# Raising the scheduling priority of turned-operand splits and of softmax normalising in a two-layer encoder trunk

## The chip, the cores and the metric

The kernel runs on one core of one Trainium2 chip. A core has five engines with a queue each: PE (TensorE, matmuls and transposes; PEld is its weight load), DVE (VectorE), ACT (ScalarE), POOL (GpSimd) and SP (SyncE, which issues transfers here). The metric is the device time of one execution in microseconds (us); lower is better. The time before is the median of three runs, 1124.85 us (1124.82 to 1125.47).

## What is computed

Two layers of a bidirectional encoder in float32, for 512 tokens of width 1024 and a memory of 256 rows. Each layer adds a normalised mixer and a normalised SwiGLU feed-forward network to x. The mixer has 12 token heads (3 key/value heads, 4 query heads on each) and 4 heads that attend to the memory. Layer 0 is banded attention within 128 tokens with a sink logit per head; layer 1 is full attention with normalised queries and keys and a rotary by row and column.

```
def reference(x, mem, ...):
    mem_n = rms_norm(mem, mem_norm_g)
    for i in range(DEPTH):                       # DEPTH = 2
        h = rms_norm(x, g_mix_pre[i])
        proj = h @ w_in[i]                       # q (768), k (192), v (192), qm (256)
        ...
        tok = mixer_a(q, k, v, sink, ...) if kind == 0 else mixer_b(q, k, v, qk_g, ...)
        mo = memory_attention(qm, km, vm)        # softmax(qm km^T / 8) vm over 256 rows
        o = jnp.concatenate([tok, mo], axis=-1) @ w_o[i]
        x = x + rms_norm(o, g_mix_post[i])
        h = rms_norm(x, g_ffn_pre[i])
        gu = h @ w_gate_up[i]
        f = (jax.nn.silu(gu[..., :D_FF]) * gu[..., D_FF:]) @ w_down[i]   # D_FF = 2816
        x = x + rms_norm(f, g_ffn_post[i])
    return x
```

## The kernel before

**Products.** Tokens are cut into four tiles of 128. Every float32 product is made of three products of a rounded form: `mm3` (L267) adds high by high, high by low and low by high. So each operand exists as a pair hi, lo. `split` (L274) makes it: ACT copies the source into hi with rounding (L280), then DVE subtracts hi from the source to give lo (L284). For some weights a flag sends hi (L278) or lo (L282) to POOL. In the profile all these splits have the lines 278 to 284, and the tile names tell them apart: whi and wlo are weights, th and tl turned probabilities or the split token output, q the split queries, a the turned rows of the feed-forward network.

**Turned operands.** A matmul contracts over partitions, so rows must be transposed first. PE transposes 128x128 blocks into a PSUM tile `tp` (tag "t", two buffers), and a split reads them out. There are three such places: `turned` (L330 and on, transposes L337) for the rows of a mixer's input, `Forms.turn` (transposes L149) for the feed-forward network, whose first products are made from sums of blocks (`Forms` keeps a1, a21, a22 and the sums S1 to S4), and `turn` (transposes L609) for a head's probabilities, which gives th and tl.

**A head.** Heads are counted through both layers here: 0 to 15 in layer 0, 16 to 31 in layer 1, the last four of each being memory heads. `score` computes the scores of one token tile (L548, L549), a row extreme nm (DVE, L554 in layer 0, L559 in layer 1), and exponentials with their sum den (ACT, L560). `score_mem` does the same for the memory heads, for two tiles at once (L578 to L580, exponentials L583). After the last tile `normalise` adds the sink term (es, L594), takes the reciprocal rd (L596) and multiplies the four tiles' probabilities p by it on POOL (L599). Then `turn` j transposes the block of keys j from all tiles that see these keys: in layer 0, j = 0 needs tiles 0 and 1 only; in layer 1 every turn needs all four. `value` multiplies th and tl by the values into one PSUM bank o (tag "pv", one buffer; L623, L624). After the last j, ACT copies half of o to tmp (L631), DVE adds the other half into tok (L632), and only then may the next head write o. The queries of the next group of four heads are projected meanwhile: the copy out of PSUM is qx (ACT, L512), a rotary follows on DVE (L423 to L444), a split gives q, its transposes are L524 and their copy qT is L525. tok is split into th (L280, L284) for the output projection.

**What sets the order.** PE's order is written by hand: in `mixer`, `put(x, f)` files each piece of work under a due time worked out from the table PACE, and the pieces are emitted in that order. On ACT, DVE, POOL and SP the build's scheduler arranges the instructions, from their priorities (by default the order of emission) and from when it takes their inputs to be there; each engine then runs its own list in order. `tc.high_priority(n)` moves the instructions emitted inside it forward by n in the scheduler's priorities.

Of the kernel before, what the change touches and what calls it, by code (L numbers as in the profile page):

```python
# [12 lines left out]
AF = mybir.ActivationFunctionType  # L13
OP = mybir.AluOpType
# [17 lines left out]
WPART = 2  # L32
BIG = 1e37
NFILL = 3
LOTS = ((0, 8), (8, 14), (14, 22))

PACE = [{'lag': 1.692, 'vlag': 0.479, 'jstep': 0.213, 'kstep': 0.375, 'klag': 0.742, 'qoff': [0.212, 0.126, 0.099], 'qlag': 1.02, 'late': 0.6, 'moff': -0.235, 'mdur': 0.562, 'mlag': 0.697, 'kw': [0, 0, 2, 0], 'mw': [2, 1, 1, 0], 'qw': [1, 0, 0, 1, 3, 3, 3, 3], 'hoff': 0, 'ow': [10.3, 10.8, 12.2, 13.2], 'ox': 11.4, 'od': 0.3, 'hstep': 0.872, 'hlag': 1.742, 'hjstep': 0.135, 'hvlag': 0.751, 'owm': [0, 0, 0, 0, 0, 0, 0, 0], 'q0step': 0.27, 'q0off': -0.032, 'q0lag': 0.919, 'm0off': -0.078, 'm0dur': 0.002, 'm0lead': 1.887, 'mlead': 1.201, 'qlead': 0.921, 'q0lead': 1.555, 'qstep': 1.002, 'tw': [0, 0, 0, 0, 0, 0, 0, 0], 'h2off': 0}, {'lag': 1.824, 'vlag': 0.535, 'jstep': 0.218, 'kstep': 0.777, 'klag': 1.715, 'qoff': [-0.027, -0.162, -0.027], 'qlag': 1.189, 'late': 2.15, 'moff': -0.088, 'mdur': 0.384, 'mlag': 1.205, 'kw': [0, 0, 0, 0], 'mw': [0, 0, 0, 0], 'qw': [0, 0, 0, 0, 0, 3, 1, 1], 'hoff': 0, 'ow': [10.2, 10.7, 12.2, 13.2], 'ox': 11.3, 'od': 0.3, 'hstep': 0.946, 'hlag': 1.847, 'hjstep': 0.295, 'hvlag': 0.568, 'owm': [0, 0, 0, 0, 0, 0, 0, 0], 'q0step': 0.718, 'q0off': -0.018, 'q0lag': 1.136, 'm0off': -1.059, 'm0dur': 0.171, 'm0lead': 2.465, 'mlead': 3.162, 'qlead': 1.895, 'q0lead': 1.42, 'qstep': 0.998, 'tw': [0, 0, 0, 0, 0, 0, 0, 0], 'h2off': 0.016}]
# [79 lines left out]
class Forms:  # L117
# [23 lines left out]
    def turn(self, t, h):  # L141
        tr, nc = self.tr, self.nc
        q, c = t // 2, slice(t % 2 * P, t % 2 * P + P)
        if q and self.s is None:
            self.new_s()
        for b in range(2):
            tp = tr.ps.tile([P, 4, P], F32, tag="t", name="tp", bufs=2)
            for k in range(4):
                nc.tensor.transpose(tp[:, k], h[:, (4 * b + k) * P:(4 * b + k + 1) * P], tr.ident)  # L149
            if q == 0:  # L150
                ks = slice(4 * b, 4 * b + 4)
                tr.split(self.a1[0][:, ks, c], self.a1[1][:, ks, c], tp)
                nc.scalar.activation(self.as1[:, ks, c], tp, AF.Copy)
                continue
            dst = (self.a21, self.a22)[b]
            tr.split(dst[0][:, :, c], dst[1][:, :, c], tp)
            if b == 0:
                a21 = self.temp("a21", 2)
                nc.scalar.activation(a21, tp, AF.Copy)
            else:  # L160
                s1 = self.temp("s1", 2)
                nc.vector.tensor_sub(s1, tp, a21)
                self.left.append((c, a21, s1))

    def finish(self):

# [13 lines left out]
class Trunk:  # L180
# [93 lines left out]
    def split(self, hi, lo, src, pool=0):  # L274
# [8 lines left out]
        else:  # L283
            nc.vector.tensor_sub(lo, src, hi.bitcast(F32))  # L284

    def split_scaled(self, hi, lo, src, r, pool=0):

        nc = self.nc
        if pool & 2:
            nc.gpsimd.tensor_scalar(hi, src, r, 1.0, op0=OP.mult, op1=OP.mult)  # L290
        else:
            nc.scalar.activation(hi, src, AF.Copy, scale=r)  # L292
        nc.vector.scalar_tensor_tensor(lo, src, r, hi.bitcast(F32), op0=OP.mult, op1=OP.subtract)
# [38 lines left out]
    def turned(self, h, his, los, t, nq=4):  # L332

        for b in range(2):
            tp = self.ps.tile([P, 4, P], F32, tag="t", name="tp", bufs=2)
            for k in range(4):
                self.nc.tensor.transpose(tp[:, k], h[:, (4 * b + k) * P:(4 * b + k + 1) * P], self.ident)  # L337
            k0 = 4 * b
            sl = (slice(None), slice(k0 % nq, k0 % nq + 4), slice(t * P, (t + 1) * P))
            self.split(his[k0 // nq][sl], los[k0 // nq][sl], tp)  # L340

    def scale_rows(self, rs, by_row=False):

# [245 lines left out]
    def normalise(self, hd):  # L589
        nc, sink, nm, den = self.nc, hd["sink"], hd["nm"], hd["den"]  # L590
        rd = self.small.tile([P, 4], F32, tag="rd", name="rd", bufs=4)
        if sink is not None:
            es = self.small.tile([P, 4], F32, tag="es", name="es", bufs=3)
            nc.scalar.activation(es, nm, AF.Exp, bias=self.sink[:, sink:sink + 1], scale=1.0)  # L594
            nc.vector.tensor_add(den, den, es)
        nc.vector.reciprocal(rd, den)  # L596
        for z, (k0, k1) in enumerate(hd["rng"]):
            n = (k1 - k0) * P
            self.pooled = nc.gpsimd.tensor_scalar(hd["p"][z][:, :n], hd["p"][z][:, :n], rd[:, z:z + 1], 1.0,  # L599
                                                  op0=OP.mult, op1=OP.mult)  # L600

    def turn(self, hd, j):
        nc = self.nc
        qs = [i for i in range(NT) if hd["rng"][i][0] <= j < hd["rng"][i][1]]
        m = len(qs)
        tp = self.ps.tile([P, 4, P], F32, tag="t", name="tp", bufs=2)
        for z, i in enumerate(qs):
            jj = j - hd["rng"][i][0]
            nc.tensor.transpose(tp[:, z], hd["p"][i][:, jj * P:(jj + 1) * P], self.ident)  # L609
        th = self.core.tile([P, 4, P], F32R, tag="th", name="th", bufs=4)  # L610
        tl = self.core.tile([P, 4, P], F32R, tag="tl", name="tl", bufs=4)
        self.split(th[:, :m], tl[:, :m], tp[:, :m])
        hd[j] = (qs[0] * P, (qs[-1] + 1) * P, th[:, :m].rearrange("p a b -> p (a b)"),
                 tl[:, :m].rearrange("p a b -> p (a b)"))

# [149 lines left out]
    def heads_out(self, l, put, xw, xs, x0, dx):  # L765
# [7 lines left out]
        def part(k):  # L773
            if k % 4 == 0:
                self.th[k // 4] = [self.hp.tile([P, 4, S], F32R, tag=f"h{k // 4}{z}", name="th", bufs=1)
                                   for z in range(2)]
            self.split(self.th[k // 4][0][:, k % 4], self.th[k // 4][1][:, k % 4], self.tok[:, k],
                       self.side(l, "tw", k))

        def prod(k, t):  # L780
            if t == len(self.po):
                self.po.append(self.bank())
                if t == 2:
                    self.held = self.turns.pop()
            self.prod(self.po[t], self.heads, KD, k, t, self.wo[k // 2])

        for k in range(KD):
            put(max(xs[k], x0 + (NFILL * k - 1.5) * dx) if k < NH // 2 else xs[k], lambda k=k: part(k))
        for k in range(NH // 2):
            for t in range(NFILL):  # L790
                put(max(x0 + (NFILL * k + t) * dx, xs[k] + 0.001 * (t + 1)), lambda k=k, t=t: prod(k, t))

# [3 lines left out]
    def mix_out(self, l, forms, resid, dst):  # L796
# [3 lines left out]
        g, gn = self.gain(a["g_mix_post"][l], "gpost"), self.gain(a["g_ffn_pre"][l], "gpre")  # L800
        po = self.po + [self.bank() for _ in range(NT - NFILL)]
        self.turns.insert(1, self.held)
        w1 = []
        for u in range(4):
            for k in (2 * u, 2 * u + 1):
                for t in range(0 if k >= NH // 2 else NFILL, NT):
                    self.prod(po[t], self.heads, KD, k, t, self.wo[u])
# [97 lines left out]
    def ffn(self, l, pools, forms, late, done):  # L905
# [92 lines left out]
        def body(f, pos, nxt, nxt2, fill):  # L998
            d = st[f]
            x = d["x"]  # L1000
            seven(f, x, "c", 1, "S2", False)
            copy(f, "u2", x)
            y = self.tagged("t")[:, :256]
            seven(f, y, "c", 0, "nS1", True)
            copy(f, "p5", y)
            if nxt is not None:
                load_b(nxt)
                prep_c(nxt)
                p1(nxt)
            else:  # L1010
                fill[0]()
            seven(f, x, "b", 1 - 1, "S3", False)
            c = d["cc"] = temp("c")
            nc.vector.tensor_add(c[:, 256:], x, d["p5"])
            if nxt is not None:
                p2(nxt)
            else:
                fill[1]()
            if nxt2 is not None:
                prep_a(nxt2)  # L1020
            seven(f, y, "b", 1, "S4", False)
            nc.vector.tensor_add(c[:, :256], y, d["u2"])
            if nxt is not None:
                prep_b(nxt)
            seven(f, x, "d", 0, "A22", False)
            s = d["s"]
            nc.scalar.activation(s[:, 256:], x, AF.Silu)
            nc.vector.tensor_mul(s, s, c)
            F[f] = hidden(pos)
            nc.scalar.activation(F[f][0], s, AF.Copy, scale=-1.0)  # L1030
            nc.vector.scalar_tensor_tensor(F[f][1], s, -1.0, F[f][0].bitcast(F32), op0=OP.mult, op1=OP.subtract)
            if nxt is not None:
                prep_d(nxt)
            st.pop(f)
# [24 lines left out]

        for c, (f0, f1) in enumerate(LOTS):  # L1060
            fs = list(range(f0, f1))
# [21 lines left out]
            for i, f in enumerate(gs):  # L1083
                more = gs[i + 1:] + [None, None]
                body(f, f - f0, more[0], more[1], [first, second])
            if c < len(LOTS) - 1:
                self.down(get, self.a["wd"][l], fs, c, o, head)
# [158 lines left out]
```

## Time and profile before

| | |
|---|---|
| Median of the runs | 1124.85 us |
| The profiled execution, its own time | 1125.38 us |
| its span in the trace | 1123.6 us |
| PE busy | 98% |
| DVE, ACT, POOL busy | 75%, 59%, 18% |
| granted PE clock, mean | 0.998 |
| PE idle in the two mixers (20 to 200 us, 565 to 745 us) | 5.7 and 6.1 us |
| PE idle in the two feed-forward networks (225 to 545, 800 to 1124 us) | 0.0 and 8.2 us, the latter nearly all at the end of the program |

PE is the engine that sets the time. The other engines matter where PE waits for them. The list of waits gives, for each pair of a PE line and the line that released it, the idle time in all, how often, and the longest. In the timeline each row has the start, the duration, the engine and line, the operation, output and inputs, and in brackets the idle time of the engine ahead of it.

### The profile page before, as it was taken

What the parts mean: (1) busy time and instruction counts of PE and PEld (TensorE: products, weight loads), DVE (VectorE), ACT (ScalarE), POOL (GpSimd) and SP (SyncE); (2) the same over time, 40 slices, a digit from 0 to 9 for tenths busy, and PEclk for the clock granted to TensorE, in tenths of its full rate; (3) what the DMA queues carried; (4) which work ended last, traced back from release to release, by engine and by line L of the source; (5) the groups of instructions that cost most, each with busy time, mean ns of one, the idle gap of its engine ahead of it and who ended that gap; (6) DMA issues with size and microseconds to landing.
All of it is one profiled execution on the core that took longest, in us unless ns stands there. A gap on an engine that the chain in (4) does not pass through costs nothing.

```text
span 1123.6 us, 19533 instructions
## 1 busy us (share of the span) xinstructions
PE 1096.6 (98%) x7463; PEld 1003.6 (89%) x7463; DVE 844.3 (75%) x1431; ACT 660.8 (59%) x1343; POOL 203.8 (18%) x348
## 2 busy tenths in 40 slices
PE   8999999999999999999999999999999999999997
PEld 7889988899889989998898888878999899899985
DVE  5688885899557867885788998758996478669854
ACT  6678984666445634663467878756665255345631
POOL 5693331102000000000343543312000000000001
PEclk9999999999999999999999999999999999999999
DMA  6521015443753382325543221145136223423243
GB/s 237 194 81 47 20 57 206 169 132 114 243 180 112 112 283 76 112 79 195 179 150 113 76 76 39 38 150 188 39 113 217 65 76 114 149 62 103 85 166 112
DMA packets 38685, 139.29 MB, mean 124 GB/s; under 512 B 4416, under 2 KB 4800, under 8 KB 38464
## 3 DMA queue, kind: packets, MB, share of 16 engines
q1 hardware_dynamic: 38448, 137.91, 36.4%
q8 instruction: 58, 0.95, 0.3%
q14 instruction: 35, 0.29, 0.1%
q10 hardware_dynamic: 144, 0.14, 0.0%
HBM read 119.16 MB, written 18.87 MB: 123 GB/s over the span
## 4 chain that ended last, share of the span: by engine, by line
PE 68%; DVE 6%; ACT 3%; POOL 2%; issue 2%; DVEq 0%; POOLq 0%; ACTq 0%
PE ps L978 12%; PE ps L979 12%; PE ps L980 12%; PE ps L271 9%; PE ps L270 9%; PE ps L272 9%; PE tp L609 1%; PE o L624 1%; PE o L623 1%; PE s L548 1%; DVE nm L559 1%; PE s L549 1%; DVE wlo L284 1%; POOL r L299 1%; ACT whi L280 1%
## 5 line engine op out<-in xcount | busy, mean ns | idle before, releaser
L280 ACT ACTIVATE whi<-raw 128x1024 fp32r<-128x1024 f32 (+2 forms) x186 | 157.9, 863 | 185.2 <-PE ps L980 81.8
L284 DVE TENSOR_TENSOR wlo<-raw,whi 128x1024 fp32r<-128x1024 f32 (+2 forms) x178 | 175.9, 998 | 74.8 <-ACT whi L280 71.7
L978 PE MATMUL ps<-sf,whi 128*128 128x256 f32 x640 | 179.9, 281 | 0.2
L979 PE MATMUL ps<-sf,wlo 128*128 128x256 f32 x640 | 179.7, 281 | 0.0
L980 PE MATMUL ps<-sf,whi 128*128 128x256 f32 x640 | 179.7, 281 | 0.0
L270 PE MATMUL ps<-whi,f 128*128 128x512 f32 x352 | 137.2, 390 | 0.0
L271 PE MATMUL ps<-wlo,f 128*128 128x512 f32 x352 | 137.1, 390 | 0.0
L272 PE MATMUL ps<-whi,f 128*128 128x512 f32 x352 | 137.0, 389 | 0.0
L980 PE MATMUL ps<-a,whi 128*128 128x256 f32 x480 | 134.4, 280 | 0.0
L978 PE MATMUL ps<-a,whi 128*128 128x256 f32 x480 | 134.3, 280 | 0.0
L979 PE MATMUL ps<-a,wlo 128*128 128x256 f32 x480 | 133.8, 279 | 0.0
L978 PEld LDWEIGHTS ps<-sf,whi 128*128 128x128 f32 x640 | 121.1, 189 | 1.1 <-ACT p L984 0.6
L979 PEld LDWEIGHTS ps<-sf,wlo 128*128 128x128 f32 x640 | 121.4, 190 | 0.5
L980 PEld LDWEIGHTS ps<-sf,whi 128*128 128x128 f32 x640 | 121.4, 190 | 0.0
L308 POOL TENSOR_SCALAR e<-sso 128x1 f32<-128x1 f32 x8 | 3.4, 424 | 566.1 <-ACT junk L303 565.9
L270 PE MATMUL ps<-whi,hT 128*128 128x256 f32 (+1 forms) x320 | 98.8, 309 | 0.9 <-ACT whi L292 0.9
L271 PE MATMUL ps<-wlo,hT 128*128 128x256 f32 (+1 forms) x320 | 93.9, 294 | 2.6 <-DVE wlo L284 1.9
L599 POOL TENSOR_SCALAR p<-p,rd 128x256 f32<-128x256 f32 (+2 forms) x128 | 78.2, 630 | 99.8 <-DVE rd L596 50.3
L272 PE MATMUL ps<-whi,hT 128*128 128x256 f32 (+1 forms) x320 | 93.7, 293 | 0.0
L979 PEld LDWEIGHTS ps<-a,wlo 128*128 128x128 f32 x480 | 90.5, 188 | 0.2
L978 PEld LDWEIGHTS ps<-a,whi 128*128 128x128 f32 x480 | 90.4, 188 | 0.2
L980 PEld LDWEIGHTS ps<-a,whi 128*128 128x128 f32 x480 | 90.1, 188 | 0.0
(201 smaller groups left out, 2735.0 us busy)
## 6 DMA issues: line engine op xcount, KB each, us to landing
raw<-in_wgu_dram SPq DMA_DIRECT2D x48, 512.0 KB, 4.4
raw<-in_wd_dram SPq DMA_DIRECT2D x44, 512.0 KB, 4.4
rb<-in_wgu_dram SPq DMA_DIRECT2D x40, 512.0 KB, 3.6
raw<-in_wo_dram SPq DMA_DIRECT2D x17, 512.0 KB, 3.6
raw<-in_wq_dram SPq DMA_DIRECT2D x16, 512.0 KB, 5.0
xt<-x SPq DMA_DIRECT2D x12, 512.0 KB, 4.5
raw<-in_wm_dram SPq DMA_DIRECT2D x8, 512.0 KB, 4.3
x<-y SPq DMA_DIRECT2D x8, 512.0 KB, 3.0
```

The costliest lines, as they stand in the source:

```text
L270: mm(out, lh, rh, start=first, stop=False)
L271: mm(out, lh, rl, start=False, stop=False)
L272: mm(out, ll, rh, start=False, stop=last)
L280: nc.scalar.activation(hi, src, AF.Copy)
L284: nc.vector.tensor_sub(lo, src, hi.bitcast(F32))
L299: g.tensor_tensor(r, r, self.mhalf[:, :r.shape[1]], op=OP.pow)
L548: nc.tensor.matmul(s[:, :n], qi, hd["ka"]()[:, k0 * P:k1 * P], start=True, stop=False)
L549: nc.tensor.matmul(s[:, :n], qi, hd["kb"]()[:, k0 * P:k1 * P], start=False, stop=True)
L599: self.pooled = nc.gpsimd.tensor_scalar(hd["p"][z][:, :n], hd["p"][z][:, :n], rd[:, z:z + 1], 1.0, op0=OP.mult, op1=OP.mult)
L978: mm(out, wh[:, s], rh, start=start and k == 0, stop=False, skip_group_check=True)
L979: mm(out, wl[:, s], rh, start=False, stop=False, skip_group_check=True)
L980: mm(out, wh[:, s], rl, start=False, stop=k == 3, skip_group_check=True)
```

## The change

The splits that read out transposes (in `Forms.turn`, `turned` and `turn`) and POOL's multiplies in `normalise` are put under `urgent()`, that is, under a scheduling priority raised by 400. Nothing is added to the program or taken from it. An attribute that nothing uses (`self.pooled`) goes.

```diff
+URGENT = 400
...
@@ Forms.turn
+            with tr.urgent():
+                if q == 0:
+                    ks = slice(4 * b, 4 * b + 4)
+                    tr.split(self.a1[0][:, ks, c], self.a1[1][:, ks, c], tp)
+                    nc.scalar.activation(self.as1[:, ks, c], tp, AF.Copy)
+                    continue
+                dst = (self.a21, self.a22)[b]
+                tr.split(dst[0][:, :, c], dst[1][:, :, c], tp)
...
+    def urgent(self):
+
+        return self.tc.high_priority(URGENT)
...
@@ turned
-            self.split(his[k0 // nq][sl], los[k0 // nq][sl], tp)
+            with self.urgent():
+                self.split(his[k0 // nq][sl], los[k0 // nq][sl], tp)
...
@@ normalise
-            self.pooled = nc.gpsimd.tensor_scalar(hd["p"][z][:, :n], hd["p"][z][:, :n], rd[:, z:z + 1], 1.0,
-                                                  op0=OP.mult, op1=OP.mult)
+            with self.urgent():
+                nc.gpsimd.tensor_scalar(hd["p"][z][:, :n], hd["p"][z][:, :n], rd[:, z:z + 1], 1.0, op0=OP.mult,
+                                        op1=OP.mult)
...
@@ turn
-        self.split(th[:, :m], tl[:, :m], tp[:, :m])
+        with self.urgent():
+            self.split(th[:, :m], tl[:, :m], tp[:, :m])
```

PE's list of instructions is the same before and after, row for row. In the changed kernel lines have moved on by 2 to 9: L280 is L282, L282 is L284, L284 is L286, L525 is L532, L559 is L566, L560 is L567, L583 is L590, L594 is L601, L599 is L607, L631 is L640, L632 is L641.

**POOL, heads 2 and 3 of layer 0.** rd_1168 belongs to head 2, whose p of the token tiles 0 to 3 are p_1073, p_1111, p_1136 and p_1165; wlo is the low part of a weight. Before:

```order
L282 TENSOR_TENSOR wlo_1632<-raw_1630,whi_1631 128x512
L599 TENSOR_SCALAR p_1073<-p_1073,rd_1168 128x256
L599 TENSOR_SCALAR p_1111<-p_1111,rd_1168 128x384
L599 TENSOR_SCALAR p_1136<-p_1136,rd_1168 128x384
L599 TENSOR_SCALAR p_1165<-p_1165,rd_1168 128x256
L282 TENSOR_TENSOR wlo_1632<-raw_1630,whi_1631 128x512
L599 TENSOR_SCALAR p_1215<-p_1215,rd_1291 128x256
```

With the change:

```order
L284 TENSOR_TENSOR wlo_1632<-raw_1630,whi_1631 128x512 x2
L607 TENSOR_SCALAR p_1073<-p_1073,rd_1168 128x256
L607 TENSOR_SCALAR p_1136<-p_1136,rd_1168 128x384
L607 TENSOR_SCALAR p_1111<-p_1111,rd_1168 128x384
L607 TENSOR_SCALAR p_1165<-p_1165,rd_1168 128x256
L607 TENSOR_SCALAR p_1215<-p_1215,rd_1291 128x256
```

Tiles 1 and 2 have changed places, as they have in each of the 32 heads, and the second half of the weight's split now stands ahead of head 2's multiplies.

**ACT, the end of layer 0's token heads and the first memory head.** den_2175 is the last token head, den_2274 the first memory head; raw_2395 is a weight. Before:

```order
L594 ACTIVATE es_2250<-nm_2174,sink_88 128x4
L280 ACTIVATE th_2269<-tp_2265 128x384
L280 ACTIVATE whi_2396<-raw_2395 128x512
L280 ACTIVATE th_2293<-tp_2289 128x384
L583 ACTIVATE p_2281,den_2274<-s_2275,nm_2273 128x256
L583 ACTIVATE p_2283,den_2274<-s_2275,nm_2273 128x256
L525 ACTIVATE qT_1715<-tp_2297 128x4x128
L280 ACTIVATE th_2318<-tp_2315 128x256
L280 ACTIVATE whi_2396<-raw_2395 128x512
```

With the change:

```order
L282 ACTIVATE th_2269<-tp_2265 128x384
L282 ACTIVATE whi_2396<-raw_2395 128x512
L567 ACTIVATE p_2246,den_2175<-p_2246,nm_2174 128x256
L282 ACTIVATE th_2293<-tp_2289 128x384
L601 ACTIVATE es_2250<-nm_2174,sink_88 128x4
L532 ACTIVATE qT_1715<-tp_2297 128x4x128
L590 ACTIVATE p_2281,den_2274<-s_2275,nm_2273 128x256
L282 ACTIVATE th_2318<-tp_2315 128x256
L590 ACTIVATE p_2283,den_2274<-s_2275,nm_2273 128x256
```

th_2269, th_2293 and th_2318 have moved forward, both parts of whi_2396 as well, and qT_1715 and th_2318 now stand ahead of the second exponential of the memory head.

**DVE, head 19 in layer 1.** tl_8011 belongs to this head's second turn, q2_7959 is the split of the next queries, tok_7503<-o_7918 is the end of the head before. Before:

```order
L444 TENSOR_TENSOR qx_7944<-qx_7944,r4_7950 128x256
L559 TENSOR_REDUCE nm_7992<-s_7994 128x1
L632 TENSOR_TENSOR tok_7503<-o_7918,tmp_8002 64x512
L284 TENSOR_TENSOR q2_7959<-qx_7944,q2_7959 128x4x64
L284 TENSOR_TENSOR tl_8011<-tp_8005,th_8010 128x512
L559 TENSOR_REDUCE nm_7992<-s_8026 128x1
```

With the change:

```order
L451 TENSOR_TENSOR qx_7944<-qx_7944,r4_7950 128x256
L566 TENSOR_REDUCE nm_7992<-s_7994 128x1
L286 TENSOR_TENSOR tl_8011<-tp_8005,th_8010 128x512
L286 TENSOR_TENSOR q2_7959<-qx_7944,q2_7959 128x4x64
L641 TENSOR_TENSOR tok_7503<-o_7918,tmp_8002 64x512
L566 TENSOR_REDUCE nm_7992<-s_8026 128x1
```

tl has moved from behind tok and q to the front, and tok stands behind both.

More of the change, by code (lines that the diff above doesn't have):

```diff
@@ L149, in turn @@
                 nc.tensor.transpose(tp[:, k], h[:, (4 * b + k) * P:(4 * b + k + 1) * P], tr.ident)
[L150 to L163, printed above, removed]
+            with tr.urgent():
[6 more added lines that the diff above has]
+                tr.split(dst[0][:, :, c], dst[1][:, :, c], tp)
+                if b == 0:
+                    a21 = self.temp("a21", 2)
+                    nc.scalar.activation(a21, tp, AF.Copy)
+                else:
+                    s1 = self.temp("s1", 2)
+                    nc.vector.tensor_sub(s1, tp, a21)
+                    self.left.append((c, a21, s1))
     def finish(self):
```

## The prediction

> **What bounds the kernel now.** I read the page first: how busy each engine is, then the list of what TensorE (PE) waits for, then the timeline at the places that the new order touches.
>
> ```profile
> span 1123.6 us, 19533 instructions
> PE 1096.6 (98%) x7463; PEld 1003.6 (89%) x7463; DVE 844.3 (75%) x1431; ACT 660.8 (59%) x1343; POOL 203.8 (18%) x348
> ```
>
> PE is busy for 1096.6 of 1123.6 us and its order is written by hand: nothing can be won except the 27 us in which it stands still. So the question for every moved instruction is whether PE waits for it, and what now comes later instead. The list of PE's waits names the lines (engine, line, releaser: total, times, longest):
>
> ```profile
> PE tp L609 <- DVE tl L284: 2.7, 6, 0.7
> PE o L623 <- DVE tok L632: 2.3, 5, 0.7
> PE tp L609 <- POOL p L599: 1.8, 3, 0.9
> ...
> PE o L624 <- DVE tl L284: 0.3, 2, 0.2
> ...
> PE tp L609 <- DVE qx L424: 0.2, 1, 0.2
> PE tp L524 <- ACT qx L512: 0.2, 1, 0.2
> ```
>
> The splits that the change brings forward (th on ACT, tl on DVE) are what PE waits for in the first and the fourth row: 2.7 + 0.3 us. The two qx waits (0.2 + 0.2) lie on the same queues and may move with them. That gives a **ceiling for the gain of 3.4 us**, 0.3% of the time. The second and third rows are work that the change can only delay: tok isn't raised, and the POOL multiplies are reordered.
>
> **The change part by part.** No instruction is added or removed, so each term is a change of a start time. The sum is made against the profiled execution's own 1125.38 us (span 1123.6 and 1.8 around it), which is 0.53 above the median 1124.85.
>
> *Normalising (POOL).* In each head the multiplies now run for token tiles 0, 2, 1, 3 instead of 0, 1, 2, 3. A layer 0 turn for keys j = 0 transposes tiles 0 and 1 only, so it now waits for the third multiply. Head 0 is a place where PE stands for exactly that:
>
> ```profile
> 71.08 2.23 POOL L599 TENSOR_SCALAR p<-p,rd 128x256 f32<-128x256 f32 x4
> 72.33 0.33 PE L609 MATMUL tp<-cst,p 128*128 128x128 f32 x1 [0.40 <-POOL p L599]
> ```
>
> Four multiplies take 2.23, one about 0.56: **+0.57**. In layer 1 a turn reads all four tiles, so there the swap costs nothing. Head 2 of layer 0 gets a second penalty: a POOL weight split (L282) that followed its four multiplies now stands ahead of them.
>
> ```profile
> 84.91 1.60 POOL L599 TENSOR_SCALAR p<-p,rd 128x384 f32<-128x384 f32 x3
> 86.48 1.48 POOL L282 TENSOR_TENSOR wlo<-raw,whi 128x512 fp32r<-128x512 f32 x1
> 86.51 0.38 PE L609 MATMUL tp<-cst,p 128*128 128x128 f32 x2
> 88.95 0.30 PE L609 MATMUL tp<-cst,p 128*128 128x128 f32 x1 [0.29 <-DVE tl L284]
> ```
>
> The last of these multiplies ended at 86.5 and the third at about 86.0. With 1.48 ahead, tile 1, now third, ends at about 87.5; PE asks for it at 86.62 (the second of the two at 86.51), moved to about 87.0 by the terms before it: **+0.4** (bounds 0 and 0.9). The other 29 heads have their multiplies ready early, since only three waits of PE on them are listed; cost nothing, cover gone only if rd comes over 1 us later.
>
> *Turned probabilities, gain.* The waits on tl and qx vanish at best: **−3.4**, all of it taken. The row at 88.95 above is one of them; the largest I can point at with nothing behind it is this one:
>
> ```profile
> 658.93 0.66 PE L609 MATMUL tp<-cst,p 128*128 128x128 f32 x4 [0.63 <-DVE tl L284]
> ```
>
> *Turned probabilities, what comes later.* ACT and DVE run one instruction after the other, so a th or tl that goes ahead pushes back everything that it passes. Five places in layer 0 put th ahead of the copy of q out of PSUM (L512), which frees the bank that the next q transposes (L524) write:
>
> ```profile
> 130.62 0.45 ACT L512 ACTIVATE qx<-ps,rq 128x256 f32<-128x256 f32 x1
> 130.97 0.48 ACT L280 ACTIVATE th<-tp 128x384 fp32r<-128x384 f32 x1
> 131.32 0.54 PE L524 MATMUL tp<-identr,q 128*128 128x128 f32 x4
> ```
>
> L512 ends at 131.07 with 0.25 to spare. Starts of neighbours on ACT are closer than their durations (0.35 from 130.62 to 130.97, for a 0.45), so a th of 0.48 costs some 0.37 of pace, and 0.12 to 0.2 is lost; five places with similar room, **+0.65** (bounds 0 and 1.8, five full th). Next, the end of layer 0's token heads, and the memory heads behind it:
>
> ```profile
> 137.85 0.68 DVE L632 TENSOR_TENSOR tok<-o,tmp 64x512 f32<-64x512 f32 x1
> 138.73 0.56 DVE L284 TENSOR_TENSOR tl<-tp,th 128x384 fp32r<-128x384 f32 x1 [0.20 <-ACT th L280]
> ...
> 138.59 0.39 PE L623 MATMUL o<-th,vs 128*128 128x256 f32 x1 [0.36 <-DVE tok L632]
> ...
> 146.24 0.47 ACT L583 ACTIVATE p<-s,nm 128x256 f32<-128x256 f32 x1
> ...
> 146.69 0.60 ACT L525 ACTIVATE qT<-tp 128x512 fp32r<-128x512 f32 x1
> 147.17 0.40 ACT L280 ACTIVATE th<-tp 128x256 fp32r<-128x256 f32 x1
> 147.43 0.65 ACT L280 ACTIVATE whi<-raw 128x512 fp32r<-128x512 f32 x1
> ...
> 146.87 0.37 PE L578 MATMUL s<-kma,qT 128*128 128x256 f32 x1
> ```
>
> PE already waits for tok at 138.59; with that tl ahead of it tok comes its 0.56 later, **+0.56**. At 146 the exponentials of the first memory head (L583), the second of which ends at 146.71, 0.16 ahead of the scores that need its bank, now stand behind qT, th and whi: 0.48 + 0.26 of pace from the rows and some 0.5 of the whi's 0.65, less 0.16, is 1.1. Part of it is hidden where PE is late already: **+0.7** (bounds 0.55 and 1.1). The same queue in layer 1 puts qT, a th and the split of tok ahead of the second L583:
>
> ```profile
> 709.28 0.48 ACT L583 ACTIVATE p<-s,nm 128x256 f32<-128x256 f32 x1
> ...
> 709.73 0.61 ACT L525 ACTIVATE qT<-tp 128x512 fp32r<-128x512 f32 x1
> 710.20 0.62 ACT L280 ACTIVATE th<-tp 128x512 fp32r<-128x512 f32 x1
> 710.68 0.66 ACT L280 ACTIVATE th<-tok 128x512 fp32r<-128x512 f32 x1
> ...
> 710.45 0.36 PE L578 MATMUL s<-kma,qT 128*128 128x256 f32 x1
> ```
>
> It ended at 709.76, 0.69 ahead of PE; 0.47 + 0.48 of pace and some 0.5 of the 0.66 go ahead: 1.5 less 0.69 is **+0.8**. At the first output of a memory head, tmp (L631) and tok now follow a th and a tl:
>
> ```profile
> 723.72 0.60 ACT L280 ACTIVATE th<-tp 128x512 fp32r<-128x512 f32 x1
> ...
> 723.73 0.69 DVE L632 TENSOR_TENSOR tok<-o,tmp 64x512 f32<-64x512 f32 x1 [1.17 <-ACT tmp L631]
> 724.45 0.69 DVE L284 TENSOR_TENSOR tl<-tp,th 128x512 fp32r<-128x512 f32 x1
> ...
> 724.48 0.50 PE L623 MATMUL o<-th,vm 128*128 128x512 f32 x1 [0.48 <-DVE tok L632]
> ```
>
> PE waits for tok here, and a 0.60 th or a 0.69 tl comes in front; DVE's idle 1.17 takes up a little: **+0.5**, and the same **+0.5** in layer 0, which has the same order. The last place is head 19 in layer 1, where tok moves behind tl and the split of q:
>
> ```profile
> 638.24 0.69 DVE L632 TENSOR_TENSOR tok<-o,tmp 64x512 f32<-64x512 f32 x1
> 638.97 0.82 DVE L284 TENSOR_TENSOR q<-qx,q 128x256 fp32r<-128x256 f32 x1
> 639.82 0.69 DVE L284 TENSOR_TENSOR tl<-tp,th 128x512 fp32r<-128x512 f32 x1
> ...
> 639.36 0.40 PE L623 MATMUL o<-th,vs 128*128 128x512 f32 x1
> ...
> 640.57 0.66 PE L609 MATMUL tp<-cst,p 128*128 128x128 f32 x4 [0.58 <-DVE tl L284]
> ```
>
> tok ended at 638.93, 0.43 before PE's use; tl (some 0.6 of its 0.69) and q (0.85 from start to start) go ahead: **+1.0**, against the 0.58 that is in the gain already. Head 18 has the same swap and more room, **+0.2**; head 22 loses an exponential and a tok to a th and a tl of such lengths, **+0.9** (bounds 0 and 1.3, both in full).
>
> The Trainium skill's page "SBUF — State Buffer" (section "Summary: rules for kernel authors") says that a DVE operation with two SBUF operands and a GpSimd operation reading SBUF block each other, whichever issues second. By that rule the split of q at 638.97, both of whose operands are in SBUF, lost some 0.4 to the normalising, and standing later it would escape it; the sum would be 0.4 lower at this head. The trace bears it out only in part: this split takes 0.82 here, but other splits of the same shape beside POOL's multiplies don't all stretch, and I keep the row's price.
>
> *Turned rows (L152–163, L337–340).* The order moves the first splits of k rows by one whi at most, the DVE work beside them is unchanged, and in both feed-forward entries the splits that PE waits for stand where they stood. **0** (bounds −0.5 and +0.3, a whole th at one of the places).
>
> **Sum.** 0.57 + 0.4 + 0.65 + 0.56 + 0.7 + 0.8 + 0.5 + 0.5 + 1.0 + 0.2 + 0.9 = 6.8 lost, 3.4 won: +3.4, so 1128.8 against the profiled execution and **1128.3 against the median**.
>
> **Rivals.** *Traded waits (no change).* PE's order is the same; if the moved exponentials, tok and qx were covered to half, 3.4 lost would meet 3.4 won: 1124.9. For it: PE waits for tok in only 5 places of 32, so most have room. Against: the places above were picked because the room is smaller than what goes ahead.
>
> *The gain without the price (faster).* At every place th and tl come earlier and the work they pass has slack, because earlier transposes also let the following heads' scores and exponentials run ahead of need. It decides if the loss is under about 1.2 in all: 1124.85 − 3.4 + 1.2 = 1122.6, and no better than 1121.5. Against: tok and L583 are waited for within 0.7 at the places quoted.
>
> The Trainium skill's page "Perfetto Trace Analysis" (section "Tensor Engine Instruction") calls the queues of ACT, DVE and GpSimd strictly first in, first out. By that rule a th waiting for its transposes also blocks ready work behind it, which speaks against this rival; the idle 0.20 before tl at 138.73, with a split of q behind it, agrees.
>
> *Losses that spread (slower still).* A late tok or L583 delays PE's next transposes, hence the next th, which now blocks more behind it. If each loss comes back half again, 10.2 − 3.4 = +6.8, so 1131.7.
>
> *The priority has no effect.* Excluded for POOL, where the order differs; for the turned rows it is my forecast.
>
> **How the numbers follow.** A measurement of this kernel can tell about 0.2% (2.25 us) from no change. Losses as summed: 0.50, between 1126 and 1130.5. Traded waits: 0.27, around 1124.9. Gain without the price: 0.13. Spreading losses: 0.10. Half of the spread and most of the traded case lie inside the range from 1123.8 (traded, with 1 us to the good) to 1131.5. Faster (under 1122.6) 0.13; within 0.2% 0.30, traded waits and the low edge of the forecast; slower (over 1127.1) 0.57.
>
> **What would show it.** In the profile of the changed kernel: the wait of L609 on tl falls from 2.7 towards 0; the wait of L623 on tok rises from 2.3 to about 5; that of L609 on POOL's p from 1.8 to about 2.8; new waits of L578 on L583 (about 1.5) and of L524 on L512. If tok and L583 don't rise, the traded or the faster case holds, and I have mistaken room for need. If waits show up in the feed-forward stretch, where PE has none now, the turned rows were not at 0.

## The result and the profile after

The changed kernel takes **1130.78 us** (median of four runs, 1129.11 to 1132.13) against 1124.84 before (1124.79 to 1125.47): slower by 0.51%, ratio 1.0051, 95% interval [1.0033, 1.0068]. The forecast was 1128.3 with a range from 1123.8 to 1131.5. The profiled execution took 1130.18, its span is 1128.4.

The page of the changed kernel, and its list of what PE waits for (engine, line, releaser: total in us, times, longest):

```profile
span 1128.4 us, 19488 instructions
PE 1097.9 (97%) x7463; PEld 1004.7 (89%) x7463; DVE 846.6 (75%) x1431; ACT 660.2 (59%) x1343; POOL 202.4 (18%) x348
```

```profile
PE o L632 <- DVE tok L641: 6.0, 9, 1.3
PE tp L617 <- POOL p L607: 3.7, 6, 1.0
PE tp L150 <- ACT a L161: 2.1, 2, 1.1
...
PE s L585 <- ACT p L590: 1.6, 2, 1.1
...
PE tp L531 <- DVE q L286: 1.0, 3, 0.5
...
PE tp L617 <- DVE tl L286: 0.4, 1, 0.4
```

The engines have as much to do as before: PE 1097.9 against 1096.6 us, the others within 1%. Of the 4.8 us by which the span has grown, 3.5 are idle time of PE (from 27.0 to 30.5); the other 1.3 are in PE's busy time, whose ends are modelled. The priority did what it says: the wait for tl fell from 2.7 to 0.4 and the waits for qx are no longer in the list. In exchange the wait for tok grew from 2.3 to 6.0, that for POOL's multiplies from 1.8 to 3.7, and a wait for the memory heads' exponentials of 1.6 is new.

PE's order is the same in both kernels, so its n-th matmul before can be set against its n-th after, and the difference of their starts (each from its span's start) shows where time is lost. The first 12 us differ by some tenths between executions of any kernel and are left out; in this pair PE comes out of them 0.5 earlier after, so that beyond them the change loses 5.3 and not 4.8. The steps of that difference over 0.1 us, at the places of the forecast and the larger ones besides:

| place (us, trace before) | what PE waits for after | forecast | measured |
|---|---|---|---|
| 72.33, head 0 | third multiply | +0.57 | +0.57 |
| 86.62, head 2 | third multiply behind a weight split | +0.4 | +1.02 |
| 90 to 131 | bank of the q transposes (the trace names it at the first place alone) | +0.65 | +0.75 in four places |
| 121.83 and 148.84 | third multiply | 0 | +0.37, +0.59 |
| 138.59 | tok behind tl, its tmp behind a th | +0.56 | +0.92 |
| 146.87 | memory exponentials behind qT and th | +0.7 | +1.28 |
| 151.70 | tok | 0 | +0.62 |
| 159.15 and 724.48 | tok behind th and tl | +0.5, +0.5 | +0.68, +0.68 |
| 619.14 | q | 0 | +0.47 |
| 630.69, head 18 | tok (the trace names a th that ended 0.12 later) | +0.2 | +0.31 |
| 639.36, head 19 | tok behind tl and q | +1.0 | +0.65 |
| 699.47 and 702.11, head 22 | an exponential, tok | +0.9 | +0.48, +0.36 |
| 710.45 | memory exponentials | +0.8 | +0.69 |
| all steps down in the heads; 5.1 of them where PE had waited for tl or qx | | −3.4 | −3.0 in layer 0, −3.5 in layer 1 |

At head 2 the timeline of the changed kernel shows the price of POOL's new order (start, duration, engine and line, in brackets the idle time ahead):

```profile
82.93 2.56 POOL L284 TENSOR_TENSOR wlo<-raw,whi 128x512 fp32r<-128x512 f32 x2
85.46 2.09 POOL L607 TENSOR_SCALAR p<-p,rd 128x256 f32<-128x256 f32 x4
...
87.14 0.33 PE L617 MATMUL tp<-cst,p 128*128 128x128 f32 x1 [0.80 <-POOL p L607]
```

The weight split of 2.56 runs first, the multiplies begin at 85.46 in place of 84.44, and the tile that PE wants is the third of the four.

At the end of layer 0's token heads:

```profile
138.97 0.55 DVE L286 TENSOR_TENSOR tl<-tp,th 128x384 fp32r<-128x384 f32 x1
139.43 0.17 DVE L603 RECIPROCAL rd<-den 128x4 f32<-128x4 f32 x1
139.52 0.65 DVE L641 TENSOR_TENSOR tok<-o,tmp 64x512 f32<-64x512 f32 x1
...
140.32 0.36 PE L632 MATMUL o<-th,vs 128*128 128x256 f32 x1 [1.29 <-DVE tok L641]
```

tmp, which tok reads, is made by ACT, before and after:

```profile
137.22 0.59 ACT L631 ACTIVATE tmp<-o 64x512 f32<-64x512 f32 x1
```

```profile
138.31 0.47 ACT L282 ACTIVATE th<-tp 128x384 fp32r<-128x384 f32 x1
138.80 0.59 ACT L640 ACTIVATE tmp<-o 64x512 f32<-64x512 f32 x1
```

tmp is there at 139.39, 1.58 later than before, and tok starts 1.67 later. PE is 0.85 late here already. Of the other 0.8, some 0.5 is a raised th that ACT now runs ahead of tmp (from 138.31 to 138.80), and only 0.1 is the tl in front of tok. PE stands for 1.29 where it stood for 0.36. Nine microseconds later the exponentials of a memory head come behind qT, which isn't raised itself, and the second of them behind a raised th as well:

```profile
147.46 0.60 ACT L532 ACTIVATE qT<-tp 128x512 fp32r<-128x512 f32 x1
147.94 0.48 ACT L590 ACTIVATE p<-s,nm 128x256 f32<-128x256 f32 x1
...
148.39 0.40 ACT L282 ACTIVATE th<-tp 128x256 fp32r<-128x256 f32 x1
148.65 0.50 ACT L590 ACTIVATE p<-s,nm 128x256 f32<-128x256 f32 x1
...
149.29 0.38 PE L585 MATMUL s<-kma,qT 128*128 128x256 f32 x1 [1.12 <-ACT p L590]
```

### The profile page after: what moved, and what is told of

Its sections match the earlier page's. It is cut to its first block, busy times and chain, and to the rows that moved or that the text cites. A ratio compares the mean times of both kernels' runs of the same rounds, so it can differ in the third digit from the quotient of the medians.

```text
span 1128.4 us, 19488 instructions
## 1 busy us (share of the span) xinstructions
PE 1097.9 (97%) x7463; PEld 1004.7 (89%) x7463; DVE 846.6 (75%) x1431; ACT 660.2 (59%) x1343; POOL 202.4 (18%) x348
## 4 chain that ended last, share of the span: by engine, by line
PE 67%; DVE 7%; ACT 3%; POOL 2%; issue 2%; DMA 0%; DVEq 0%; POOLq 0%; SPq 0%; ACTq 0%
PE ps L987 12%; PE ps L988 12%; PE ps L989 12%; PE ps L273 9%; PE ps L272 9%; PE ps L274 9%; PE tp L617 1%; PE o L632 1%; PE o L633 1%; DVE nm L566 1%; DVE wlo L286 1%; DVE tl L286 1%; PE s L555 1%; PE s L556 1%; POOL r L305 1%
## 5 line engine op out<-in xcount | busy, mean ns | idle before, releaser
L282 ACT ACTIVATE whi<-raw 128x1024 fp32r<-128x1024 f32 (+2 forms) x186 | 158.3, 864 | 187.0 <-PE ps L989 81.9
L286 DVE TENSOR_TENSOR wlo<-raw,whi 128x1024 fp32r<-128x1024 f32 (+2 forms) x178 | 175.4, 995 | 75.8 <-ACT whi L282 71.6
L607 POOL TENSOR_SCALAR p<-p,rd 128x256 f32<-128x256 f32 (+2 forms) x128 | 76.4, 617 | 107.4 <-DVE rd L603 67.8
```

The costliest lines, as they stand in the source:

```text
L282: nc.scalar.activation(hi, src, AF.Copy)
```

## The experiments

Each kernel was timed beside the kernel before on the same chip. All start from the kernel before, unless they are called the whole change. The theory, called the queue theory in the expectations, is the one of the prediction: PE loses where a raised split stands ahead of work that PE needs sooner.

**One part alone: normalising.**

```diff
@@ normalise, only here
+            with self.urgent():
```

> Only the multiplies of the normalising are raised. Their order becomes 0, 2, 1, 3 in each head; nothing moves on ACT or DVE. Queue theory (what PE lost, it lost to tok and to exponentials that stand behind raised th and tl): only the swap is left, +0.6 at head 0 and up to 0.6 more at the places where the changed kernel waits longer for POOL (3.7 against 1.8 us in the list of waits); 0.5 to 1.5 us slower than before. Rival (POOL sets the loss): most of it, 3 to 5 us slower. Rival (no part of it costs by itself): within 0.5 us.

1124.91 us against 1124.29, ratio 1.0008 [0.9999, 1.0017]: +0.6, where the interval still includes no change. Nothing but POOL's order differs, and PE's starts step by 0.56 at head 0 and by 0.19 at 616.42; no other step up is over 0.15 beyond the first 12 us. With th and tl at their old places, the third multiply is in time at all other heads. The ten runs fall into two groups, to which the last section returns: six from 1124.56 to 1124.91 and four from 1125.86 to 1126.10.

**One part alone: th and tl.**

```diff
@@ turn, only here
+        with self.urgent():
+            self.split(th[:, :m], tl[:, :m], tp[:, :m])
```

> Only th and tl are raised. Queue theory: 3.5 to 5 us slower than before; PE's wait for tok about 5.5 us, for the exponentials of the memory heads about 1.5, for tl under 0.7. The weight split of POOL ahead of head 2's multiplies comes with this part: 0.3 to 0.6 there. Rival (POOL sets the loss): 0 to 1 us slower.

1128.89 against 1124.29, ratio 1.0038 [1.0024, 1.0052]: +4.6, of the whole change's 5.9. PE's waits:

```profile
PE o L629 <- DVE tok L638: 6.1, 9, 1.3
PE tp L614 <- POOL p L604: 2.0, 4, 0.9
...
PE s L583 <- ACT p L588: 1.5, 2, 1.1
...
PE tp L614 <- DVE tl L285: 0.4, 1, 0.4
```

All but the wait for POOL is as in the whole change. At head 2 PE loses 0.45: the weight split ahead of the multiplies, without the swap. So that move on POOL comes from raising th and tl; with the normalising alone the split stays behind the multiplies.

**One part alone: turned rows.**

```diff
@@ Forms.turn and turned, only here
+            with self.urgent():
```

> Only the splits of turned rows (both places) are raised. Queue theory: within 0.7 us of before, no wait of PE in its list changes by over 0.4 us. Rival (the turned rows delay the softmax work around them): over 1 us slower, with new waits between 20 and 70 us or at the feed-forward entries.

1125.20 against 1124.29, ratio 1.0008 [0.9998, 1.0017]. Beyond the first 12 us no wait of PE changes by over 0.3 (`a` at the feed-forward entries from 1.8 to 2.1), yet the median is 0.9 up, a little over what was expected, where the interval still includes no change. Six of its ten runs have a mean granted clock of 0.998 or 0.999 and lie between 1124.46 and 1125.33, the other four 0.996 and 1125.52 to 1126.08; the last section returns to this.

**What PE waits for, raised as well.** The whole change, with tmp, tok and the memory heads' exponentials under the same priority.

```diff
@@ value
+        with self.urgent():
+            nc.scalar.activation(tmp[here], o[there], AF.Copy)
+            nc.vector.tensor_add(self.tok[here, hg // 2], o[here], tmp[here])
@@ score_mem
+            with self.urgent():
+                nc.scalar.activation(p[:, :NMEM], s[:, z], AF.Exp, ...)
```

> The whole change, and tmp, tok and the exponentials of the memory heads raised as well. Queue theory: the wait for tok falls from 6.0 to 1.5 us or less, that for the memory heads' exponentials from 1.6 to under 0.3, the wait for tl stays under 1; the time is 4 to 6.5 us below that of the change, 1124 to 1127. Rival (POOL sets the loss): the wait for p stays and the time stays within 1 us of the change. Rival (later tl in exchange): tok's wait goes, tl's comes back to 2.5, and the time is 2 to 4 us below that of the change.

1129.32 against 1124.29, ratio 1.0042 [1.0027, 1.0057]: only some 1 us of the loss is gone (less still against the change's second measurement, below), not the 4 to 6.5 expected. The waits themselves did as the theory has it:

```profile
PE tp L618 <- POOL p L608: 4.6, 6, 1.0
...
PE s L555 <- ACT p L567: 1.7, 1, 1.7
PE o L633 <- DVE tok L643: 1.6, 3, 0.7
...
PE s L585 <- ACT p L591: 0.5, 1, 0.5
```

tok's wait falls from 6.0 to 1.6 and the memory exponentials' from 1.6 to 0.5, but POOL's p, whose exponentials aren't raised, is waited for 0.9 longer, and one token head's exponential 1.7 in place of 0.5. So the first expectation was right on the waits it named and wrong on the time. In part that is what tok pushes back in its turn, which it left out. In part it is PE's clock: set against the trace of the change, PE's starts of this profiled execution lose 1.6 between 72.9 and 75 us, where its trace has a stretch at half the granted clock (last section). Over the whole program they gain 2.3; without that stretch it would be 3.9, just short of the low end expected. The mean clocks of these runs, 0.995 to 0.997, are also lower than those of the kernel before.

**One turn of four.** Only the turn for keys j = 1 is raised.

```diff
@@ turn
+        with self.tc.high_priority(URGENT if j == 1 else 0):
             self.split(th[:, :m], tl[:, :m], tp[:, :m])
```

> th and tl are raised for the second turn of each head alone (keys j = 1). It is the split that stands behind the tok of the head before. Queue theory: this quarter of the turns has nearly the whole loss, 3 to 4.5 us slower than before, with PE's wait for tok at 5 or more and the wait for tl lower than before. Rival (each raised split costs its share): 1 to 1.3 us slower, a quarter to a third of what all four turns cost.

1129.32 against 1124.60, ratio 1.0042 [1.0028, 1.0056]: +4.7, as much as all four turns together cost and a little above the 4.5 named. (In the memory heads, which have two turns, j = 1 is every other one. The turn j = 0 alone was not run.)

```profile
PE o L629 <- DVE tok L638: 5.5, 8, 1.2
...
PE tp L614 <- DVE tl L285: 1.4, 3, 0.7
```

**The other end of the head.** Only the turns j = 2 and 3 are raised (`j >= 2` in the same place).

> th and tl are raised for the turns j = 2 and 3 alone, half of them in layer 0 and in layer 1's token heads. Queue theory: these pass no tok that PE waits for, so the wait for tok stays at 2.3 and the time within 0.8 us of before. Rival (each raised split costs its share): 1.8 to 2.3 us slower.

1124.57 against 1124.60, ratio 0.9997 [0.9988, 1.0007]: no loss. The wait for tok is 2.9, slightly over the 2.3 expected, and that for tl 3.0. A wait of 0.9 for the memory exponentials is new; the waits for qx are no longer in the list. In PE's starts the steps over 0.15 come to 2.8 lost and 2.4 won.

**Token heads alone** (`hd["hg"] < NH` in the same place).

> th and tl are raised in the token heads alone, not in the memory heads. Queue theory: the two waits for tok at the first output of the memory heads (0.69 each) don't grow, the one for the memory exponentials in layer 1 falls; 1.3 to 2.2 us less than with all turns raised, so 2.4 to 3.3 slower than before. Rival (the loss sits with the token heads alone): the same as with all turns raised within 0.5.

1127.56 against 1124.60, ratio 1.0029 [1.0018, 1.0041]: +3.0, 1.6 less than with the memory heads. The wait for tok is 4.9 in place of 6.1. The wait for the memory exponentials stays at 1.6, which I had expected to fall: the th in front of them is one of a token head.

**Token heads, with tmp and tok of all heads.** Nothing else is raised.

```diff
@@ turn
+        with self.tc.high_priority(400 if hd["hg"] < NH else 0):
@@ value
+        with self.tc.high_priority(400):
+            nc.scalar.activation(tmp[here], o[there], AF.Copy)
+            nc.vector.tensor_add(self.tok[here, hg // 2], o[here], tmp[here])
```

> th and tl raised in the token heads alone, tmp and tok raised as much in all heads, no normalising and no turned rows raised. Queue theory: tok stands ahead of tl at every place, so the waits for tok and for tl are both under 1.5 us; 0 to 2 us faster than before. Rival (what is raised always delays something else that PE waits for, as the exponentials did when tok was raised with everything): 1 to 3 us slower.

1124.41 against 1124.60, ratio 0.9999 [0.9990, 1.0008]: the 3 us of the run before are recovered, and nothing is won. The waits for tok and tl are down to 1.3 and 1.2, but one exponential pays. This is ACT of that kernel, and PE behind it:

```profile
697.53 0.59 ACT L639 ACTIVATE tmp<-o 64x512 f32<-64x512 f32 x1
698.15 0.60 ACT L281 ACTIVATE th<-tp 128x512 fp32r<-128x512 f32 x1
698.65 0.68 ACT L565 ACTIVATE p<-s,nm 128x512 f32<-128x512 f32 x1
...
699.47 0.50 PE L553 MATMUL s<-ka,qT 128*128 128x512 f32 x1 [1.75 <-ACT p L565]
```

tmp and th, both raised, run ahead of the exponential that frees the score bank, and PE stands for 1.75. Up to there PE had gained 1.4 in layer 1 over the kernel before. Right behind it this execution loses another 1.6 in a stretch at half the clock (last section).

**The whole change without turn j = 1.**

```diff
@@ turn
+        with self.tc.high_priority(0 if j == 1 else URGENT):
```

> The whole change, with the turn j = 1 of every head left at its old priority. Queue theory: the wait for tok is back at 2 to 3 us, and what is left over the kernel before is the swap of the normalising (0.6) and the memory exponentials; 0.5 to 2 us slower than before, 4 or more below the whole change. Rival (the parts act together, and any raised turn costs with the swap): over 3 us slower than before.

1126.88 against 1124.64, ratio 1.0019 [1.0010, 1.0029]: +2.2, a little above the expected end. The wait for tok is 3.9, not 2 to 3. Of the 2.4 that PE's starts lose in the profiled execution beyond the first 12 us, 1.5 are lost at 218 to 220, in the feed-forward network and in a stretch at half the clock (last section), which leaves 0.9 for the queues and the swap. Nine of its ten runs have a clock of 0.997 or 0.998, one 0.995.

**Raised where it pays.** Put together from the steps seen in the runs above.

```diff
@@ turn
+        up = (j >= 2 and hd["hg"] < 10) if hd["sink"] is not None else hd["hg"] < 8
+        with self.tc.high_priority(URGENT if up else 0):
+            self.split(th[:, :m], tl[:, :m], tp[:, :m])
@@ value
+        up = hd["sink"] is None and hg < 8
+        with self.tc.high_priority(URGENT if up else 0):
+            nc.scalar.activation(tmp[here], o[there], AF.Copy)
+            nc.vector.tensor_add(self.tok[here, hg // 2], o[here], tmp[here])
```

> th and tl raised only where the runs so far show a gain: in layer 0 the turns j = 2 and 3 of the first ten heads; in layer 1 all turns of the first eight heads, with their tmp and tok raised as much. Nothing else is raised. Queue theory: the waits for tl (2.7) and tok (2.3) shrink by 2 us in all, with no new wait over 0.5; 1 to 2 us faster than before. Rival (a gain at one place is lost at the next): within 0.5 us of before.

**1122.33** against 1124.64, ratio 0.9980 [0.9970, 0.9989]: 2.3 us faster than the kernel before, a little more than the 1 to 2 expected, and some 7 to 8 faster than the change (1129.65 and 1130.78 in two measurements).

```profile
PE o L630 <- DVE tok L641: 2.0, 4, 0.7
...
PE tp L614 <- DVE tl L285: 1.9, 3, 0.8
...
PE s L583 <- ACT p L588: 0.6, 1, 0.6
```

The two waits shrink by 1.1 in all, less than the 2 expected, and the two for qx (0.4) are gone; the one for the memory exponentials is 0.6 where 0.5 was the bound named. That is a net 0.9, while the paired starts show a gain of 2.4 beyond the first 12 us: 1.2 in the mixer of layer 0 and 1.6 in that of layer 1, less 0.4 lost between. The list counts less, because a step can be larger than the idle time that goes (0.75 at 640.57 for a listed 0.58).

**The change again, and the change with the tiles in their old order.**

```diff
@@ normalise, in the whole change
+            with self.tc.high_priority(URGENT + 40 * (NT - z)):
```

> The change itself once more, for its spread. If the spread of 3 us comes from a halved clock after a stretch of idle PE (seen in three profiles so far), its runs fall into groups: near 1129.5 with a mean granted clock of 0.998 or 0.999, and 1.2 to 1.7 us higher for each such stretch, with 0.997 or less. Rival (waits that differ from run to run): no relation of time and clock.

> The whole change, but the multiplies of a head keep the order of the tiles 0, 1, 2, 3 (each is raised a little less than the one ahead of it); all else stands as in the change. Queue theory: the two waits for the third multiply in layer 0 (0.57 each at heads 0 and 2) go and little else, so 1 to 1.6 us less than the change itself in runs of equal clock; with the shorter idle at head 0 there are fewer runs of a low clock. Rival (the order of the multiplies is a detail that POOL's slack hides): within 0.5 us of the change.

The change: 1129.65 against 1124.45, ratio 1.0048 [1.0035, 1.0060]. With the order kept: 1128.52, ratio 1.0035 [1.0021, 1.0049], 1.1 less. PE's starts, paired with those of the change's first trace, step back by 0.57 at head 0, 0.56 at head 2, and, which I hadn't expected, 0.37 and 0.57 at 121.83 and 148.84: 0.34 comes back at 125.67, so the swap costs 1.7 in this pair of traces and 1.1 by the medians when th and tl are raised too, against 0.6 alone.

## Why the prediction was right, and where it was off

The sign, the range and the mechanism held. The sum gave +3.4 against the profiled execution; span against span it is +4.8, and the medians differ by 5.9. That it came so near is in part luck. It had 6.8 lost and 3.4 won, where the steps over 0.1 add up to 11.9 and 6.9: both sides were too small, and the errors took each other off. Some of that is the same time twice, lost at one place and won back at the next.

**"What bounds the kernel now"**, a ceiling for the gain and tok and POOL as what can only get worse, is what the list of waits after shows. One of the signs named didn't come: the list has no new wait of the q transposes for qx. Those places lost 0.75 in steps, as priced (0.65), but two of them (110.74 and 117.95) no longer wait for qx and win 0.7 back.

**"Turned probabilities, what comes later"** was the right step for most of the loss, and the runs narrow it down. Raising th and tl alone gives 4.6 of 5.9 (5.2 in the second measurement); raising j = 1 alone gives as much, raising j = 2 and 3 nothing. The rival of losses in proportion to what is raised falls with that. That it is the queue, and nothing in the splits themselves, is shown by tmp and tok raised with them: the loss of 3.0 goes.

Its terms were too small in layer 0. At 138.59 (0.92 for 0.56) I had the wrong queue: I priced the tl in front of tok on DVE, which held it for 0.1, and left out the th in front of tmp on ACT, which brought some 0.5. The size came near by luck. At 146.87 (1.28 for 0.7) I took off a part for PE being late already; PE is 1.17 late there, but the second exponential ends 2.44 later than before. The tok at 151.70 (0.62) I had not priced. In layer 1 the terms were about right or too large: head 19 lost 0.65 for 1.0.

On head 19 the rule of the Trainium skill's page "SBUF — State Buffer" (section "Summary: rules for kernel authors"), that a DVE operation with two SBUF operands and a GpSimd operation reading SBUF block each other, would have given 0.6, nearer to the 0.65 than my 1.0. The split of q there took 0.82 before and 0.41 after:

```profile
643.46 0.41 DVE L286 TENSOR_TENSOR q<-qx,q 128x256 fp32r<-128x256 f32 x1
643.88 0.69 DVE L641 TENSOR_TENSOR tok<-o,tmp 64x512 f32<-64x512 f32 x1
...
641.37 3.06 POOL L607 TENSOR_SCALAR p<-p,rd 128x512 f32<-128x512 f32 x4
```

But POOL was still multiplying when this split ran (641.37 to 644.43), as it was before, so the split didn't escape by standing behind POOL's work. That the rule is the reason for the 0.82 is not shown, and the nearer number may be luck.

Against the rival of a gain without a price I read the idle 0.20 before tl at 138.73 as ready work, a split of q, that a th held up. That reading was wrong: ACT writes the high part of that q from 138.59 to 139.01, so the split on DVE wasn't ready. The row says nothing on the rival; the runs do.

**"Normalising"**: the swap's 0.57 at head 0 is exact. At head 2 (1.02 for 0.4) two things were off. I had PE arrive later by about 0.4, but it had won back about half of head 0's 0.57 by then and was 0.3 late. And the third multiply came later than the 1.48 put in front of it: set against PE's start just before head 0, it ended 1.8 later. "The other 29 heads have their multiplies ready early" held for the normalising alone but not for the whole change: two more places in layer 0 (121.83, 148.84) wait for the third multiply, and with the tiles in their old order these waits go.

**"The gain"**: the 3.4 were there, and more: −6.5 in steps over 0.1 in the heads, of which a part only takes back what a late tok had cost just before. The losses of the table, 10.4, and 1.5 in smaller steps stand against it.

**"Turned rows: 0"**: beyond the first 12 us no wait of PE moved by over 0.3, as forecast, but the runs of that part alone were 0.9 up [−0.2, +1.9], for which the last section has a possible reason and no proof.

Of the rivals, "traded waits" describes two of the experiments (j = 2 and 3; token heads with tok), not the change. "The gain without the price" holds where it is steered to those places: 1122.33, by chance close to the 1122.6 that was given for another kernel. "Losses that spread" was near in the number for the runs at the top of the change's spread; that losses breed losses there is not shown.

## What to carry to other kernels

Where engines run in order, a higher priority for what the bound engine waits for is a trade, not a gift: list what each raised instruction passes, and compare the slack of what is passed with its length. The place matters more than the amount: here raising one turn in four was enough for the whole loss, and raising about half of the turns, chosen from the traces, gave a faster kernel. List the passed work on every engine that feeds the wait, and not only on the one whose instruction the wait names. When a batch is normalised or split piece by piece, look at the order in which a scheduler emits the pieces, for a consumer that needs the first two waits for the third if it comes in between.

## What the hardware showed that I had not expected

Three of the profiled executions have a stretch in which PE is granted half its clock for 3.4 us, each beginning within 1.1 us after a stretch of mostly idle PE. This is the whole change without turn j = 1, in slices of a microsecond at the feed-forward entry of layer 0 (length; busy time of PE, PEld, DVE, ACT, POOL with counts; granted PE clock; DMA share; GB/s):

```profile
213.00:214.00 1.00, 1.00 (x11) 1.00 (x10) 1.00 (x2) 0.00 (x0) 0.00 (x0) 1.00 0.73 287
214.00:215.00 1.00, 0.44 (x4) 0.24 (x3) 1.00 (x3) 0.14 (x1) 0.00 (x0) 1.00 0.18 74
215.00:216.00 1.00, 0.48 (x4) 0.42 (x4) 1.00 (x3) 0.46 (x1) 0.00 (x0) 1.00 0.79 156
216.00:217.00 1.00, 0.40 (x4) 0.25 (x3) 1.00 (x3) 0.79 (x2) 0.00 (x0) 1.00 0.93 373
217.00:218.00 1.00, 1.00 (x8) 1.00 (x7) 1.00 (x3) 0.77 (x2) 0.00 (x0) 0.57 0.99 406
218.00:219.00 1.00, 1.00 (x6) 1.00 (x6) 1.00 (x3) 1.00 (x3) 0.00 (x0) 0.50 0.29 115
219.00:220.00 1.00, 1.00 (x7) 1.00 (x6) 1.00 (x3) 1.00 (x3) 0.00 (x0) 0.50 0.00 0
220.00:221.00 1.00, 1.00 (x8) 1.00 (x7) 1.00 (x3) 0.90 (x2) 0.00 (x0) 0.72 0.00 0
221.00:222.00 1.00, 1.00 (x11) 1.00 (x10) 1.00 (x3) 0.00 (x0) 0.00 (x0) 1.00 0.00 0
```

The clock is back at 1.00 after 3.4 us; the missing shares (0.43 + 0.50 + 0.50 + 0.28) are 1.7 us. Measured on PE's starts, set against those of the kernel before, such a stretch costs 1.5 here and 1.6 in the two other cases. The same three slices of half-idle PE stand in the trace of the turned rows alone, with no halving behind them:

```profile
214.00:215.00 1.00, 0.43 (x4) 0.23 (x2) 1.00 (x3) 0.15 (x1) 0.00 (x0) 1.00 0.14 57
215.00:216.00 1.00, 0.50 (x4) 0.42 (x4) 1.00 (x3) 0.45 (x1) 0.00 (x0) 1.00 0.76 176
216.00:217.00 1.00, 0.40 (x4) 0.27 (x3) 1.00 (x3) 0.81 (x2) 0.00 (x0) 1.00 1.00 344
217.00:218.00 1.00, 1.00 (x11) 1.00 (x10) 1.00 (x3) 0.88 (x3) 0.00 (x0) 1.00 0.93 360
```

They stand in the traces of the kernel before and of the change as well, without a halving. So the halvings seen follow such stretches, but a stretch doesn't always bring one. The other two cases stand behind the 1.75 us of idle PE at 698 in the run of token heads with tok, and behind two waits for POOL around 70 in the run with tok raised on top of the change.

One such stretch costs about what separates the runs of a kernel from each other. Of the change's nine runs, the five with a mean clock of 0.998 or 0.999 took 1129.11 to 1130.18, the four with 0.997 took 1130.61 to 1132.13; a halving of 1.7 us is 0.0015 of the span. The normalising alone, which adds little but 0.56 of idle PE at head 0, has the same two groups: six runs at 0.998 or 0.999 and four, 1 to 1.5 us longer, at 0.997, where the twenty of the kernel before beside it all have 0.998 or 0.999; the turned rows alone show the same, less sharply. In any 3.4 us beyond the first 15, PE was busy for at least 0.55 before, and for 0.46 at head 0 in the change. That fits a kernel whose longer waits set off more halvings, and it could account for some of the difference between the profile's +4.8 and the median's +5.9; 0.5 of that lies in the first 12 us, where the trace of the kernel before was the longer. It isn't settled. The five runs with turn j = 1 alone all have a clock of 0.998 and still spread from 1128.18 to 1130.26. The mean clock also counts the end of the program, where PE is done and the clock is halved in every trace from a moment that differs by some us (the run with the tiles in order has 0.997 with no halving before its end), no profile of the change itself has caught a halving, and no kernel here was made to add idle time and nothing else.
